# Split weights in rows of 260 elements instead of 256, in a one-core trunk kernel

## The chip, the cores and the metric

The kernel runs on one core of one Trainium2 chip. The metric is the time of one execution on the device, in microseconds (us); shorter is better. Below, PE is TensorE (matmuls; its weight loads are listed as PEld), DVE is VectorE, ACT is ScalarE, POOL is GpSimd, and SP is SyncE, whose queue issues all DMAs of this kernel. SBUF is the on-chip memory with 128 partitions, PSUM the memory that matmuls accumulate in.

## The reference: one step of a hybrid trunk layer

A batch of 288 tokens (a prompt of 256 and 8 samples of 4 new tokens) with 2048 channels passes one layer, all in float32:

```python
h = rmsnorm(x, norm1_g)
proj = h @ w_in + b_in                      # 2048 x 3072: a, gate, z
u = a * sigmoid(gate)                       # 1024 channels
c = silu(layernorm(depthwise_conv31(u), ln_g, ln_b))
d = windowed_mean(z, 2 | 4 | 8 | 16) - z    # 1024 channels in 4 groups
p = (d @ pool_w[group]) * pool_scale        # 4 x (256 x 256)
x = x + concat([c, p]) @ w_out              # 2048 x 2048
h2 = rmsnorm(x, norm2_g)
x = x + square(relu(h2 @ w_ff1)) @ w_ff2    # 2048 x 8192, 8192 x 2048
y = rmsnorm(x, norm_f)
```

The convolution and the windows also read the samples' stored history, and the new histories are outputs beside y. The three large weight arrays and pool_w come to some 175 MB, each element of which is read once.

## The kernel before

**Layout.** Activations are channel-major: channels lie on the partitions, the 288 tokens along the row. An activation tile is 128 channels by 288 tokens, 1152 bytes in each partition. Weights come in blocks of 1 MB: 1024 rows by two times 128 columns, held as `raw`, a tile of [128, 8, 256] float32 (8 values of k, 256 columns). SP's queue issues the loads in the order of use; three raw tiles rotate (`wraw`).

**The split.** TensorE's fast float32 format keeps fewer bits, so every float32 operand of a large product is cut in two parts that add up to it: hi, the rounded value, and lo, the rest. `split` (L202) does this for weights: for each half of a raw block, that is 4 values of k by 256 columns, ACT copies the half into a `whi` tile (L213), and DVE, or POOL for some of them before the MLP, subtracts: `wlo` = raw - `whi` (L214). Four `whi` and four `wlo` tiles rotate (`wspl`, L92). A tile has 4 rows of 256 elements in each partition: 4096 bytes.

**The products.** `gemm` (L223) makes 2 x 128 output channels for all tokens from n values of k. For each k and each half m of the 256 columns it issues three matmuls of 128 weight columns and 288 moving columns: hi weights times hi activations (L233), hi weights times lo activations (L234), lo weights times hi activations (L235). Each has its own weight load. Behind its matmuls `gemm` asks the generator `weight_groups` for the next group's splits, so that these run during the current group. There are 8112 such matmuls: 1152 of the input projection, 48 of the pooling groups, 768 of the output projection and 6144 of the MLP. The MLP runs in four chunks of 2048 inner channels; in each, 8 groups of w_ff1 products read the tiles `ah` and `al`, then 8 groups of w_ff2 products read 32 tiles `fh` and `fl`, which the first product's evictions made (L452 to L457). The activation tiles come from a pool of 40 rotating buffers (`actp`, L93), with two smaller sets that are reused later for parts of `ah` and `al`.

**Other work.** In the first 240 us the convolution taps on DVE (L316), the pooling windows on POOL and DVE (L347 to L362) and the LayerNorm run beside the input and output projections. `rsqrt_rows` (L177) turns sums of squares into 1 / sqrt on every partition. It is called four times. It keeps four small vectors `s[0]` to `s[3]` of 3 elements on 96 partitions (L183): DVE writes `s[0]` (L184), ACT takes the square root into `s[1]` (L185) and in two of the calls loads the next function's table with a small activation that reads a column of `s[1]` (L164), DVE takes the reciprocal into `s[2]` (L188) and makes one Newton step (L189 to L191).

**Order.** The engines' programs and all waits between them come from a tile framework: it takes the operations as written, orders them by priority and by a simulated timeline, and puts waits where two operations touch the same part of a buffer. Work inside `later()` gives way to other work that is ready. Each engine then runs its list in order.

Of the kernel before, what the change touches and what calls it, by code (L numbers as in the profile page):

```python
# [9 lines left out]
F32 = mybir.dt.float32  # L10
F32R = mybir.dt.float32r
# [3 lines left out]
PSUM = bass.MemoryType.PSUM  # L15

P = 128
D = 2048
SEQ = 256
NB, NS = 8, 4  # L20
T = SEQ + NB * NS
TB = T // 3
# [7 lines left out]
N8 = DC // P  # L30
# [9 lines left out]

# groups of two 128-column results of the input projection, in order: a convolution tile's pair
# (a_i, gate_i), or a pooling group, the widest windows first
SEQUENCE = [("conv", 0), ("conv", 1), ("conv", 2), ("conv", 3)]
# [5 lines left out]
def weight_blocks():  # L49
    """Blocks of 1024 rows and 2 x 128 columns of the weights in the order of their use:  # L50
    (array, first row, the first columns)."""
    for kind, i in SEQUENCE:
        cols = (i * P, DC + i * P) if kind == "conv" else (2 * DC + 2 * i * P, 2 * DC + (2 * i + 1) * P)
        for r in range(0, D, 1024):
            yield "w_in", r, cols
    yield "pool_w", 0, (0, P)
    for r in (DC, 0):
        for c in range(0, D, 256):
            yield "w_out", r, (c, c + P)
    for ch in range(0, DFF, FCH):  # L60
        for c in range(ch, ch + FCH, 256):
            for r in range(0, D, 1024):
                yield "w_ff1", r, (c, c + P)
        for c in range(0, D, 256):
            for r in range(ch, ch + FCH, 1024):
                yield "w_ff2", r, (c, c + P)


# of 8 lo parts, how many GpSimd computes
SHARE = {"first": 2, "second": 4, "conv": 7, "pool": 5, "pool_w": 3, "w_out": 6}  # L70

# per-channel vectors, [P, columns]: channel = column * P + partition
VEC = (("norm1_g", 16), ("b_in", 24), ("conv_b", 8), ("ln_g", 8), ("ln_b", 8), ("pool_scale", 8), ("norm2_g", 16), ("norm_f", 16))
# [9 lines left out]
def trunk_kernel(ctx: ExitStack, tc: tile.TileContext, io):  # L83
    """Activations are channel-major: [channel on the partitions, token]. Tokens: the prompt's
    256, then 8 x 4 of the samples. Every float32 operand of a large product is split exactly in
    two float32r parts (12 bits each): w x = wh xh + wh xl + wl xh, in float32 accumulation."""
    nc = tc.nc

    const = ctx.enter_context(tc.tile_pool(name="const", bufs=1))
    rowp = ctx.enter_context(tc.tile_pool(name="rowp", bufs=4))  # L90
    wraw = ctx.enter_context(tc.tile_pool(name="wraw", bufs=3))
    wspl = ctx.enter_context(tc.tile_pool(name="wspl", bufs=4))  # L92
    actp = ctx.enter_context(tc.tile_pool(name="actp", bufs=40))  # L93
    tmpp = ctx.enter_context(tc.tile_pool(name="tmpp", bufs=8))
# [7 lines left out]
    def nm(s):  # L102
        seen[s] = seen.get(s, 0) + 1
        return f"{s}{seen[s]}"

    @contextmanager
    def later(by=LATER):
        """Work that gives way to all else that is ready."""
        tc.cur_priority += by
        yield  # L110
        tc.cur_priority -= by
# [18 lines left out]

# [1 line left out]
    vec = const.tile([P, NV], F32, name="vec")  # L132
    xT = const.tile([P, KT, T], F32, name="xT")
    u_all = const.tile([P, N8, UL], F32, name="u_all")
    z_all = const.tile([P, N8, ZL], F32, name="z_all")
# [6 lines left out]
    def load(cuts=((0, 8),), x_cuts=()):  # L142
        """The next 1 MB of weights; at the start in pieces, with pieces of x between them"""
        raw = wraw.tile([P, 8, 256], F32, name=nm("wr"), tag="wr")
        src = io["w"][next(blocks)]
        for j, (k0, k1) in enumerate(cuts):
            if j < len(x_cuts):
                a, b = x_cuts[j]
                nc.sync.dma_start(xT[:, a:b, :], io["xT"][:, a:b, :])
            nc.sync.dma_start(raw[:, k0:k1, :], src[:, k0:k1, :])  # L150
        return raw
# [10 lines left out]
    def load_table(func, src):  # L162
        """The function's table is loaded once src is there."""
        nc.scalar.activation(few[: src.shape[0], :], src, func)  # L164
# [12 lines left out]
    def rsqrt_rows(parts, scale, after=None):  # L177
        """PSUM [P, T], on every partition: 1 / sqrt(scale * sum over parts and partitions + eps)."""
        pt = ms("pt", 3)
        for j in range(3):  # L180
            for n, t in enumerate(parts):
                nc.tensor.matmul(pt[:TB, j : j + 1], t[:, j * TB : (j + 1) * TB], ones[:, 0:1], start=n == 0, stop=n == len(parts) - 1)  # L182
        s = [const.tile([TB, 3], F32, name=nm("st")) for _ in range(4)]  # L183
        nc.vector.tensor_scalar(s[0], pt[:TB, 0:3], scale, EPS, op0=ALU.mult, op1=ALU.add)  # L184
        nc.scalar.activation(s[1], s[0], AF.Sqrt)  # L185
        if after is not None:
            load_table(after, s[1][:, 0:1])
        nc.vector.reciprocal(s[2], s[1])  # L188
        nc.vector.tensor_tensor(s[3], s[2], s[2], op=ALU.mult)  # L189
        nc.vector.scalar_tensor_tensor(out=s[3], in0=s[3], scalar=-0.5, in1=s[0], op0=ALU.mult, op1=ALU.mult)  # L190
        nc.vector.scalar_tensor_tensor(out=s[2], in0=s[3], scalar=1.5, in1=s[2], op0=ALU.add, op1=ALU.mult)  # L191
        dg = tmp("dg")
        for j in range(3):
            nc.vector.tensor_scalar(dg[:TB, j * TB : (j + 1) * TB], ident, s[2][:, j : j + 1], None, op0=ALU.mult)
        pr = ms("pr")
        nc.tensor.matmul(pr[:, :T], ones[:TB, :], dg[:TB, :], start=True, stop=True)
        return pr

# [1 line left out]
    turn = {"n": 0}  # L200

    def split(raw, share=0, cut=4):  # L202
        """[P, 8, 256] -> get(k, m): the parts of 128 columns; `share` of 8 on GpSimd"""
        parts = []
        for h in range(2):
            hi = wspl.tile([P, 4, 256], F32R, name=nm("whi"), tag="whi")
            lo = wspl.tile([P, 4, 256], F32R, name=nm("wlo"), tag="wlo")
            turn["n"] += share
            eng = nc.gpsimd if turn["n"] >= 8 else nc.vector
            turn["n"] %= 8  # L210
            for k in range(0, 4, cut):
                src = raw[:, 4 * h + k : 4 * h + k + cut, :]
                nc.scalar.copy(hi[:, k : k + cut, :], src)  # L213
                eng.tensor_tensor(lo[:, k : k + cut, :], src, hi[:, k : k + cut, :].bitcast(F32), op=ALU.subtract)  # L214
            parts.append((hi, lo))

        def get(k, m):
            hi, lo = parts[k // 4]
            return hi[:, k % 4, m * P : (m + 1) * P], lo[:, k % 4, m * P : (m + 1) * P]

        return get

    def gemm(banks, rhs, m_outer=False):  # L223
        """banks[m] = sum over k of w(k, m)^T rhs[k]; the next group's weights are split meanwhile"""
        n = len(rhs)
        gets = ready.pop()
        order = [(k, m) for k in range(n) for m in range(len(banks))]
        if m_outer:
            order.sort(key=lambda km: km[1])
        for k, m in order:  # L230
            (xh, xl), b = rhs[k], banks[m][:, :T]
            wh, wl = gets[k // 8](k % 8, m)
# [7 lines left out]

# [1 line left out]
    hx = []  # L242
# [8 lines left out]
    def weight_groups():  # L251
        """Per group of products, get(k, m) for each block of 8 k, in the order of the products."""
        yield [split(raw0, SHARE["first"], 2), split(raw1, SHARE["first"], 2)]
# [5 lines left out]
        for _ in range(8):  # L259
            get = split(load(), SHARE["w_out"])  # L260
# [8 lines left out]

# [1 line left out]
    scratch = z_all[:].rearrange("p k t -> p (k t)")[:, 0 : 5 * 2 * T].rearrange("p (n k t) -> p n k t", n=5, t=T)  # L271
# [15 lines left out]

# [1 line left out]
    cs = []  # L289
# [38 lines left out]

# [1 line left out]
    dd = {}  # L330
# [39 lines left out]

# [1 line left out]
    mixp = {}  # L372
# [9 lines left out]

# [1 line left out]
    pmean = ms("pmean")  # L384
# [24 lines left out]

# [1 line left out]
    for g in range(8):  # L411
# [4 lines left out]

# [1 line left out]
    x1 = []  # L418
# [20 lines left out]

# [1 line left out]
    r2 = row("r2")  # L441
# [34 lines left out]

# [1 line left out]
    rf = rsqrt_rows([ssf, qf], 1.0 / D)  # L478
# [62 lines left out]
```

## Time and profile before

| | |
|---|---|
| median of 3 runs | 1126.65 us (1126.13 to 1128.41) |
| profiled execution, first to last instruction | 1125.9 us |
| PE busy | 1094.4 us (97%), 8190 matmuls |
| DVE busy | 677.1 us (60%) |
| ACT busy | 468.7 us (42%) |
| POOL busy | 188.8 us (17%) |
| mean DMA rate | 166 GB/s |
| mean granted TensorE clock | 0.987 of full speed |

In the profile's tables a row of instructions reads: line, engine, operation, the tile written and those read (buffer numbers left out), shapes as partitions x elements, the count behind an x, then busy time in us and the mean duration of one in ns, then the idle time of that engine just before, with what ended most of it. In a table by stretches each engine has its busy time and the number of its instructions in brackets; PEclk is the clock that TensorE was granted. A timeline row begins with the start in us and the duration. The digits of a row such as "PE 7998..." are the busy tenths of 40 equal slices of the span. Matmuls are pipelined, so the durations of neighbouring ones overlap and the spacing of their starts is what counts.

### The profile page before, as it was taken

To read this page: it belongs to the slowest core of one execution; us is meant where nothing else is said; L and a number is where in the kernel's file an instruction comes from. 1 tells how busy PE (TensorE), PEld (TensorE's weight loads), DVE (VectorE), ACT (ScalarE), POOL (GpSimd) and SP (SyncE) were. 2 spreads that over 40 slices of the span, in tenths; PEclk is the share of its full clock that TensorE was granted. 3 is DMA by queue.
4 is the path that set the end of the run, shared out by engine and by line. 5 is a ranking of instruction groups with operands and counts; after the bars stand their busy time and mean duration, and the time that the engine had idled before them with its cause. 6 is when DMAs were issued, how large, how long until landed. Compare 5 with 4: busy or idle time off the path is not lost.

```text
span 1125.9 us, 19336 instructions
## 1 busy us (share of the span) xinstructions
PE 1094.4 (97%) x8190; PEld 1089.8 (97%) x8190; DVE 677.1 (60%) x983; ACT 468.7 (42%) x643; POOL 188.8 (17%) x149
## 2 busy tenths in 40 slices
PE   7998898999999999999999999999999999999995
PEld 7998898999999999999999999999999999999995
DVE  7999999788755544445555444455444445555554
ACT  6443345356544433334444333344433334444441
POOL 4789886612200000000000000000000000000000
PEclk9999998989999999999999999999999999999998
DMA  8554438534445444444445454444444454545432
GB/s 298 191 175 164 148 115 222 184 113 166 172 150 177 160 171 167 158 179 154 184 153 183 152 182 156 174 163 167 170 160 178 153 184 151 183 155 175 162 113 84
DMA packets 31910, 187.01 MB, mean 166 GB/s; under 512 B 3408, under 2 KB 7760, under 8 KB 10448
## 3 DMA queue, kind: packets, MB, share of 16 engines
q1 hardware_dynamic: 31824, 185.78, 47.0%
q8 instruction: 64, 1.05, 0.4%
q14 instruction: 22, 0.18, 0.0%
HBM read 181.49 MB, written 4.28 MB: 165 GB/s over the span
## 4 chain that ended last, share of the span: by engine, by line
PE 86%; DVE 9%; POOL 2%; issue 2%; DMA 1%; ACT 0%; SPq 0%; DVEq 0%; POOLq 0%
PE ac L233 29%; PE ac L234 28%; PE ac L235 28%; DVE pc L316 3%; DVE wlo L214 1%; POOL wlo L214 1%; DVE d L354 1%; DVE ssc L397 1%; DVE d L351 1%; DMA xT<-in_xT 1%; POOL s L347 0%; DVE d L359 0%; DVE z_all L283 0%; PE pt L182 0%; DVE xT L481 0%
## 5 line engine op out<-in xcount | busy, mean ns | idle before, releaser
L213 ACT CAST whi<-wr 128x1024 fp32r<-128x1024 f32 (+1 forms) x342 | 355.0, 1040 | 562.8 <-PE ac L234 543.6
L214 DVE TENSOR_TENSOR wlo<-wr,whi 128x1024 fp32r<-128x1024 f32 (+1 forms) x295 | 364.7, 1236 | 371.8 <-ACT whi L213 371.7
L233 PE MATMUL ac<-ah,whi 128*128 128x288 f32 x1024 | 302.7, 296 | 0.0
L233 PE MATMUL ac<-fh,whi 128*128 128x288 f32 x1024 | 302.4, 295 | 0.0
L234 PE MATMUL ac<-al,whi 128*128 128x288 f32 x1024 | 301.2, 294 | 0.0
L234 PE MATMUL ac<-fl,whi 128*128 128x288 f32 x1024 | 301.2, 294 | 0.0
L235 PE MATMUL ac<-fh,wlo 128*128 128x288 f32 x1024 | 299.3, 292 | 0.0
L235 PE MATMUL ac<-ah,wlo 128*128 128x288 f32 x1024 | 298.8, 292 | 0.0
L235 PEld LDWEIGHTS ac<-fh,wlo 128*128 128x128 f32 x1024 | 193.1, 189 | 0.0
L235 PEld LDWEIGHTS ac<-ah,wlo 128*128 128x128 f32 x1024 | 192.9, 188 | 0.0
L234 PEld LDWEIGHTS ac<-fl,whi 128*128 128x128 f32 x1024 | 192.7, 188 | 0.0
L234 PEld LDWEIGHTS ac<-al,whi 128*128 128x128 f32 x1024 | 192.4, 188 | 0.1
L233 PEld LDWEIGHTS ac<-ah,whi 128*128 128x128 f32 x1024 | 192.1, 188 | 0.1
L233 PEld LDWEIGHTS ac<-fh,whi 128*128 128x128 f32 x1024 | 192.0, 188 | 0.0
L233 PE MATMUL ac<-hh,whi 128*128 128x288 f32 x384 | 113.6, 301 | 7.7 <-DVE tg L302 6.6
L214 POOL TENSOR_TENSOR wlo<-wr,whi 128x1024 fp32r<-128x1024 f32 (+1 forms) x47 | 112.3, 2400 | 34.0 <-ACT whi L213 31.4
L234 PE MATMUL ac<-hl,whi 128*128 128x288 f32 x384 | 114.9, 301 | 3.0 <-DVE hl L246 2.9
L235 PE MATMUL ac<-hh,wlo 128*128 128x288 f32 x384 | 114.2, 301 | 1.5 <-DVE wlo L214 1.4
L316 DVE SCALAR_TENSOR_TENSOR pc<-u_all,vec,pc 128x256 f32<-128x256 f32 x232 | 100.1, 479 | 1.3
L233 PEld LDWEIGHTS ac<-hh,whi 128*128 128x128 f32 x384 | 73.3, 193 | 8.4 <-issue 7.0
L234 PEld LDWEIGHTS ac<-hl,whi 128*128 128x128 f32 x384 | 74.3, 194 | 4.1 <-DVE hl L246 4.1
L235 PEld LDWEIGHTS ac<-hh,wlo 128*128 128x128 f32 x384 | 74.1, 194 | 2.3 <-DVE wlo L214 2.2
(115 smaller groups left out, 875.5 us busy)
## 6 DMA issues: line engine op xcount, KB each, us to landing
wr<-in_w SPq DMA_DIRECT2D x167, 1024.0 KB, 4.9
xT<-in_xT SPq DMA_DIRECT2D x8, 288.0 KB, 5.7
wr<-in_w SPq DMA_DIRECT2D x8, 256.0 KB, 5.6
out_u_out<-u_all SPq DMA_DIRECT2D x1, 1208.0 KB, 8.6
out_yT<-xT SPq DMA_DIRECT2D x2, 576.0 KB, 2.9
u_all<-in_hist_c SPq DMA_DIRECT2D x8, 136.0 KB, 5.8
out_z_out<-z_all SPq DMA_DIRECT2D x1, 668.0 KB, 7.4
z_all<-in_hist_p SPq DMA_DIRECT2D x4, 152.0 KB, 4.0
```

What stands on the lines that cost most here:

```text
L213: nc.scalar.copy(hi[:, k : k + cut, :], src)
L214: eng.tensor_tensor(lo[:, k : k + cut, :], src, hi[:, k : k + cut, :].bitcast(F32), op=ALU.subtract)
L233: nc.tensor.matmul(b, wh, xh, start=k == 0, stop=False)
L234: nc.tensor.matmul(b, wh, xl, start=False, stop=False)
L235: nc.tensor.matmul(b, wl, xh, start=False, stop=k == n - 1)
L316: nc.vector.scalar_tensor_tensor(out=dst, in0=up[:, w : w + SEQ], scalar=cwv[:, w : w + 1], in1=pc, op0=ALU.mult, op1=ALU.add)
L351: nc.vector.scalar_tensor_tensor(out=d[:, w - 1 : SEQ], in0=s[:, PH + w - 1 : ZO], scalar=1.0 / w, in1=z[:, PH + w - 1 : ZO], op0=ALU.mult ...
L354: nc.vector.scalar_tensor_tensor(out=samples(d[:, SEQ:T], NS), in0=ss[:, :, PH:], scalar=1.0 / w, in1=zs[:, :, PH:], op0=ALU.mult, op1=ALU ...
L397: nc.vector.tensor_tensor(ssc, ssc, q, op=ALU.add)
```

## The change

The tiles `whi` and `wlo` get 260 elements in a row instead of 256, of which the first 256 are used. A row then takes 1040 bytes and a tile 4160, so that the starts of rows and buffers fall on all multiples of 16 bytes modulo 256. The raw tile, the transfers, the instructions and their number of elements stay as they are; the written operand of L213 and two operands of L214 are now four separate runs of 256 elements. The eight weight tiles take 512 bytes more in each partition. To make room, the four small vectors of `rsqrt_rows` become slices of one tile. Apart from these lines only comments differ.

```diff
     wspl = ctx.enter_context(tc.tile_pool(name="wspl", bufs=4))
+    WROW = 256 + 4
...
-        s = [const.tile([TB, 3], F32, name=nm("st")) for _ in range(4)]
+        st = const.tile([TB, 4, 3], F32, name=nm("st"))
+        s = [st[:, n, :] for n in range(4)]
...
-            hi = wspl.tile([P, 4, 256], F32R, name=nm("whi"), tag="whi")
-            lo = wspl.tile([P, 4, 256], F32R, name=nm("wlo"), tag="wlo")
+            hi = wspl.tile([P, 4, WROW], F32R, name=nm("whi"), tag="whi")[:, :, 0:256]
+            lo = wspl.tile([P, 4, WROW], F32R, name=nm("wlo"), tag="wlo")[:, :, 0:256]
```

## The prediction

> **What bounds the kernel now.** I read the page first, for the busy shares, the waits before the split instructions and the chain that ended last.
>
> ```profile
> span 1125.9 us, 19336 instructions
> PE   7998898999999999999999999999999999999995
> PEclk9999998989999999999999999999999999999998
> PE 86%; DVE 9%; POOL 2%; issue 2%; DMA 1%; ACT 0%; SPq 0%; DVEq 0%; POOLq 0%
> L213 ACT CAST whi<-wr 128x1024 fp32r<-128x1024 f32 (+1 forms) x342 | 355.0, 1040 | 562.8 <-PE ac L234 543.6
> L214 DVE TENSOR_TENSOR wlo<-wr,whi 128x1024 fp32r<-128x1024 f32 (+1 forms) x295 | 364.7, 1236 | 371.8 <-ACT whi L213 371.7
> ```
>
> TensorE (PE) carries 86% of the chain. From the eighth slice on it is nearly always full, at the full granted clock. ScalarE (ACT) waits 543.6 us for PE to release a `whi` buffer, and VectorE (DVE) 371.7 us for ACT. So in the long stretch the splitting engines are early, and the time is the number of matmuls times their spacing, start to start. Next I read the busy time by stretches: the cold start, the busy first part, the whole MLP, and four equal stretches of the MLP.
>
> ```profile
> core 0: us, PE busy (x) PEld busy (x) DVE busy (x) ACT busy (x) POOL busy (x), PEclk, DMA share, GB/s
> 17.20:20.40 3.20, 3.20 (x13) 3.20 (x14) 3.20 (x7) 3.20 (x8) 0.64 (x1) 0.50 1.04 417
> 40.00:200.00 160.00, 149.69 (x1094) 148.74 (x1093) 156.56 (x322) 65.48 (x94) 134.29 (x90) 0.97 0.49 164
> 301.60:1111.30 809.70, 809.70 (x6160) 809.59 (x6159) 397.04 (x470) 323.48 (x418) 1.02 (x1) 1.00 0.46 162
> 404.50:502.50 98.00, 98.00 (x745) 98.00 (x744) 45.05 (x48) 33.74 (x36) 0.00 (x0) 1.00 0.45 162
> 507.00:605.00 98.00, 98.00 (x748) 98.00 (x747) 49.42 (x60) 41.88 (x59) 0.00 (x0) 1.00 0.47 166
> 606.00:704.00 98.00, 98.00 (x748) 98.00 (x747) 45.53 (x49) 33.89 (x35) 0.00 (x0) 1.00 0.46 164
> 808.00:906.00 98.00, 98.00 (x745) 98.00 (x744) 45.53 (x49) 33.90 (x35) 0.00 (x0) 1.00 0.46 163
> ```
>
> In the MLP, 809.7 us over 6160 PE instructions is 131.4 ns each. Now the cold start, where the granted clock is 0.50; from 18.29 to 20.21 lie eight matmuls, two of them in the row "x2" left out here.
>
> ```profile
> 18.29 0.44 PE L234 MATMUL ac<-hl,whi 128*128 128x288 f32 x1
> 18.53 0.44 PE L235 MATMUL ac<-hh,wlo 128*128 128x288 f32 x1
> ...
> 20.21 0.42 PE L234 MATMUL ac<-hl,whi 128*128 128x288 f32 x1
> ```
>
> 1.92 us over eight is 240 ns. Half of that, 120 ns, is what the same 288 columns would take at the full clock if nothing else came in. They take 131.4. So about 11 ns of each of the 8112 matmuls on split weights, 89 us in all, is an excess that appears at the full clock alone. It bounds what any arrangement of addresses could win.
>
> Is that excess a matter of addresses? From the code: a `whi` or `wlo` tile has 4096 bytes in a partition, its rows 1024, a half row 512, so all weight operands start at one residue modulo 256. A moving tile has 1152 bytes, 4.5 times 256, so neighbours alternate between two residues, 128 apart. The relation "moving start minus weight start, modulo 256" has two values today, 0 and 128. In the chunks' second products `fh` and `fl` change places in this respect: their 32 tiles come out of a ring of 40 buffers, so chunks 0 and 2 have mostly `fh` on the weights' residue, chunks 1 and 3 `fl`. Of three products two move `fh`. The stretches above show just this: 745 matmuls in 98 us in chunks 0 and 2 (404.5 and 808), 748 in chunk 1 (606) at the same clock and the same load on ACT and DVE. That is 131.54 against 131.02 ns. The relation counts, by 0.5 ns between its two values.
>
> The last view is the timeline of PE behind a stall.
>
> ```profile
> 110.42 0.37 PE L233 MATMUL ac<-hh,whi 128*128 128x288 f32 x1 [2.99 <-DVE tg L302]
> ...
> 110.89 0.29 PE L233 MATMUL ac<-hh,whi 128*128 128x288 f32 x1
> 111.02 0.30 PE L234 MATMUL ac<-hl,whi 128*128 128x288 f32 x1
> 111.16 0.30 PE L235 MATMUL ac<-hh,wlo 128*128 128x288 f32 x1
> 111.29 0.30 PE L233 MATMUL ac<-hh,whi 128*128 128x288 f32 x1
> 111.43 0.31 PE L234 MATMUL ac<-hl,whi 128*128 128x288 f32 x1
> 111.57 0.30 PE L235 MATMUL ac<-hh,wlo 128*128 128x288 f32 x1
> ...
> 112.11 0.30 PE L233 MATMUL ac<-hh,whi 128*128 128x288 f32 x1
> ...
> 113.70 0.30 PE L233 MATMUL ac<-hh,whi 128*128 128x288 f32 x1
> ```
>
> The first nine matmuls from 110.89 take 1.22 us, 135.6 ns each, although nothing waits. The next twelve, from 112.11, take 1.59 us, 132.5 each. So the spacing depends on how the two streams of reads stand to each other in time too: after a disturbance it is worse, then it settles.
>
> **The change, part by part.** *Addresses of the weights.* A row becomes 1040 bytes (4 x 256 + 16), a tile 4160 (16 x 256 + 64). Row k of buffer t then starts at 64t + 16k modulo 256: sixteen residues; `wlo` starts four tiles (65 x 256) behind `whi`, on the same ones. Moving tiles keep their two residues. So the relation, constant for hundreds of matmuls today, moves by 16 bytes with every k, that is every six matmuls. No row shows the other fourteen relations. The bounds: at best the whole excess goes, -89 us; at worst PE is always as it is in the nine matmuls behind the stall, 135.6 against 131.3 (the mean of the four stretches), 4.3 ns x 8112 = +35 us. The restart rows are nearest, since there too a settled spacing is broken. If every one of the 1352 steps (8112 / 6) cost what a restart costs, 9 x 4.3 = 39 ns, that would be 52 us, above the cap of 35. But a step is 16 bytes, an eighth of the 128 that part the two known relations; I take an eighth of the cost. 52 / 8 = **+6.6 us**.
>
> The Trainium skill, "SBUF — State Buffer", section "Who interferes with whom", gives TensorE two read ports, one for the moving operand and one for the weights, and says that it never waits on anyone. By that the spacing couldn't depend on a relation of addresses, and this term would be 0 instead of +6.6; the stretches with 745 and 748 speak against it as a strict rule.
>
> *The split instructions.* Each of the 342 copies and 342 subtractions writes (the subtraction also reads) four rows instead of one run. In the MLP nothing of it shows: the idle times of 543.6 and 371.7 us before them hide it. Without that cover, between 40 and 200 us, DVE is busy 156.56 of 160 us.
>
> ```profile
> L214 DVE TENSOR_TENSOR wlo<-wr,whi 128x1024 fp32r<-128x1024 f32 x12 | 17.5, 1460 | 0.5 <-ACT whi L213 0.5
> L481 DVE TENSOR_TENSOR xT<-xT,pr 128x1152 f32<-128x1152 f32 x2 | 2.6, 1348 | 0.0
> L481 DVE TENSOR_TENSOR xT<-xT,pr 128x576 f32<-128x576 f32 x2 | 1.5, 746 | 0.0
> L481 DVE TENSOR_TENSOR xT<-xT,pr 128x288 f32<-128x288 f32 x1 | 0.5, 455 | 0.8 <-PE pr L196 0.8
> L213 ACT CAST whi<-wr 128x512 fp32r<-128x512 f32 x8 | 4.9, 608 | 1.0 <-DMA wr<-in_w 0.9
> ```
>
> L481 already reads an operand in rows (one row of 288 repeated): one row 455 ns, two 746, four 1348, about 300 for each further row, less than a row alone. I take 0. The far end: if each of three row starts cost an instruction's fixed part (ACT 608 ns for 512 elements, 1040 for 1024, so 176 ns fixed), that would be 0.53 us on each of DVE's 12 splits of this stretch, +6 us. A gain is excluded: the elements stay the same. GpSimd (POOL) does 47 of the subtractions; DVE and not POOL fills this stretch, so they get 0 too.
>
> *The four small vectors of `rsqrt_rows` in one tile.* Same instructions. A cost arises only if the reciprocal (L188) now also waits for the table load that reads a neighbouring slice.
>
> ```profile
> L188 DVE RECIPROCAL st<-st 96x3 f32<-96x3 f32 x4 | 0.7, 168 | 0.8 <-ACT st L185 0.8
> L164 ACT ACT_TABLE_LOAD x4 | 5.1, 1283 | 0.8 <-PEq L523 0.7
> L164 ACT ACTIVATE few<-st 96x1 f32<-96x1 f32 x2 | 0.4, 202 | 0.0
> ACT hh L245 <- DMA xT<-in_xT: 2.2, 2, 2.1
> ```
>
> Two of the four calls load a table: at most 2 x (1.28 + 0.20) = +3.0 us. Behind the reciprocal stand the rest of DVE's queue and the matmul L196. I take 0: `hh` reads slices of one tile that eight transfers fill and waited for transfers only twice, so waits go by slices. No DMA is added or moved on any queue.
>
> Sum: 6.6 + 0 + 0 against the profiled execution's span of 1125.9 gives 1132.5; the median of the three runs, 1126.65, stands 0.75 above it, so **1133 us**.
>
> **The rivals.** *Slower through broken settling (forecast), 0.46.* For it: the restart. Against it: it is scaled from a single kind of disturbance. 1129 to 1150 us.
>
> *Faster: today's two relations are poor ones, 0.34.* If the mean over sixteen relations lies below today's mean, PE gains on every matmul. For it: 11 ns of excess, and two relations that already differ by 0.5 ns. Against it: nothing shows a relation that is much better. Priced at three times the difference seen, 1.6 ns x 8112 = -13 us: 1114 us. It decides from a mean spacing below 131.0 ns (0.28 ns x 8112 = 2.3 us, the 0.2% that a measurement of this kernel can tell from no change).
>
> *No effect: the fourteen new relations average to the old two, 0.14.* The mean over a rotation is what two opposite points of it give, if the excess comes from two streams that pass each other a fixed number of times. 1126.6 us. This is also where the skill's rule of independent ports, quoted above, would lead.
>
> *Slower by the small terms alone, 0.06.* DVE's rows or the wait for the table: +3 to +9 us, 1130 to 1136, seen before 300 us and not in the MLP.
>
> **How the numbers follow.** Slower 0.46 + 0.06 = 0.52, same 0.14, faster 0.34. The time is the forecast's, 1133. The range has to hold both signs: down to 1110, a little past the faster rival's 1114, and up to 1150, two thirds of the way to the cap 1162 of PE always unsettled; about 0.06 is left out below and 0.1 above.
>
> **What would show it.** In the four MLP stretches of 98 us, 745 to 748 matmuls today: about 742 by the forecast, above 752 by the faster rival, 745 to 748 without effect. L213 and L214 in the MLP stay near 1.04 and 1.24 us and still wait for PE and ACT. L188 keeps its wait of 0.2 to 0.3 us a call. Cold matmuls stay at 240 ns. The prediction is wrong if spacing falls, or if the time goes in the first 300 us.

## The result and the profile after

The changed kernel takes 1133.2 us (median of 4 runs, 1130.89 to 1135.58) against 1126.42 before: 1.0059 times as long, 95% interval 1.0043 to 1.0076. It is slower, by about 6.8 us.

From the page of the changed kernel: the span, the granted clock in 40 slices, the chain by engine, and the copies and subtractions of the split (L215 and L216 are L213 and L214 of before).

```profile
span 1133.9 us, 19336 instructions
PEclk8999998989999999999999999999999999999998
PE 89%; DVE 6%; POOL 2%; issue 1%; DMA 1%; ACT 0%; SPq 0%; DVEq 0%; POOLq 0%
L215 ACT CAST whi<-wr 128x1024 fp32r<-128x1024 f32 (+1 forms) x342 | 354.7, 1038 | 568.7 <-PE ac L236 552.2
L216 DVE TENSOR_TENSOR wlo<-wr,whi 128x1024 fp32r<-128x1024 f32 (+1 forms) x295 | 364.4, 1235 | 376.8 <-ACT whi L215 376.6
L216 POOL TENSOR_TENSOR wlo<-wr,whi 128x1024 fp32r<-128x1024 f32 (+1 forms) x47 | 113.5, 2427 | 35.0 <-ACT whi L215 32.4
```

The split costs what it did: 1038 ns against 1040 on ACT, 1235 against 1236 on DVE, and on POOL, which does no subtractions in the MLP, 2427 against 2400. ACT waits longer for PE (552.2 us against 543.6), so PE has become slower, and the others wait for it. The table by stretches of the changed kernel has the whole MLP in its first row, then the four stretches of 98 us:

```profile
302.60:1119.00 816.40, 816.40 (x6158) 816.29 (x6158) 397.26 (x470) 323.23 (x418) 1.00 (x1) 1.00 0.46 160
404.50:502.50 98.00, 98.00 (x741) 98.00 (x740) 45.04 (x49) 33.78 (x35) 0.00 (x0) 1.00 0.48 168
507.00:605.00 98.00, 98.00 (x741) 98.00 (x740) 49.30 (x62) 41.85 (x59) 0.00 (x0) 1.00 0.47 166
606.00:704.00 98.00, 98.00 (x741) 98.00 (x740) 45.08 (x49) 33.85 (x35) 0.00 (x0) 1.00 0.48 166
808.00:906.00 98.00, 98.00 (x741) 98.00 (x740) 45.61 (x49) 33.20 (x36) 0.00 (x0) 1.00 0.47 162
```

The MLP takes 816.4 us instead of 809.7: +6.7 us at the same full clock, within 0.1 us of what the medians differ by. A stretch now counts 741 matmuls, where there were 745 or 748. Such a count takes in also the two or three matmuls that lie across the ends of the stretch, so 98 us divided by it comes out some 0.4 ns too small. From here on a spacing is taken from the starts in the trace: over the whole MLP 132.7 ns instead of 131.6 (132.67 and 131.55; four longer steps near the start of the MLP, which all kernels have, are left out). The difference between the chunks is gone too, since each chunk now runs through all relations. The profiled spans differ by 8.0 us. Of the rest, 1.3 us, 1.0 lies before the MLP, which starts at 302.6 instead of 301.6; the first slice had a lower granted clock in this profile (digit 8 against 9).

Each engine's instructions are the same as before, in the same order and with as many waits. As far as the medians go, the time went into the spacing of matmuls in the MLP.

### The profile page after: what moved, and what is told of

Read it like the earlier page. It is cut to its first block, busy times and chain, and to the rows that moved or that the text cites. A ratio compares the mean times of both kernels' runs of the same rounds, so it can differ in the third digit from the quotient of the medians.

```text
span 1133.9 us, 19336 instructions
## 1 busy us (share of the span) xinstructions
PE 1103.4 (97%) x8190; PEld 1098.7 (97%) x8190; DVE 673.8 (59%) x983; ACT 468.6 (41%) x643; POOL 189.9 (17%) x149
## 4 chain that ended last, share of the span: by engine, by line
PE 89%; DVE 6%; POOL 2%; issue 1%; DMA 1%; ACT 0%; SPq 0%; DVEq 0%; POOLq 0%
PE ac L237 30%; PE ac L235 29%; PE ac L236 29%; DVE pc L318 2%; POOL wlo L216 1%; DVE wlo L216 1%; DVE ssc L399 1%; DMA xT<-in_xT 1%; PE pt L183 1%; POOL s L349 1%; DVE d L353 0%; DVE d L356 0%; DVE xT L483 0%; DVE z_all L285 0%; DVE c L392 0%
## 5 line engine op out<-in xcount | busy, mean ns | idle before, releaser
L215 ACT CAST whi<-wr 128x1024 fp32r<-128x1024 f32 (+1 forms) x342 | 354.7, 1038 | 568.7 <-PE ac L236 552.2
L216 DVE TENSOR_TENSOR wlo<-wr,whi 128x1024 fp32r<-128x1024 f32 (+1 forms) x295 | 364.4, 1235 | 376.8 <-ACT whi L215 376.6
L237 PE MATMUL ac<-fh,wlo 128*128 128x288 f32 x1024 | 303.2, 296 | 0.0
L237 PE MATMUL ac<-ah,wlo 128*128 128x288 f32 x1024 | 302.8, 296 | 0.0
L216 POOL TENSOR_TENSOR wlo<-wr,whi 128x1024 fp32r<-128x1024 f32 (+1 forms) x47 | 113.5, 2427 | 35.0 <-ACT whi L215 32.4
```

What stands on the lines that cost most here:

```text
L237: nc.tensor.matmul(b, wl, xh, start=False, stop=k == n - 1)
```

## The experiments

"Relation" is, as in the prediction, the moving operand's start minus the weights' start, modulo 256. A hi activation and its lo neighbour always differ by 128, so a kernel that holds its relations has two. By the addresses in the built programs, three in four hi operands have the one in some chunks, and three in four the other in the rest.

Unless more are named, a time below is one execution. Single times of the kernel before lie between 1125.2 and 1128.7 us. The MLP itself takes 809.7, 809.7 and 809.6 us in the profiles of three kernels that hold the same relations (the kernel before and two of the runs below). So the comparisons go by the MLP.

### The relation held at other values: shifts by 32, 64 and 96 bytes

The weights stay in rows of 256; a gap ahead of the activation pool moves all activations (here by 32 bytes).

```diff
+    padp = ctx.enter_context(tc.tile_pool(name="padp", bufs=1))
+    gap = padp.tile([P, 8], F32, name="gap")     # 16 for 64 bytes, 24 for 96
+    nc.vector.memset(gap[:, 0:1], 0.0)
     actp = ctx.enter_context(tc.tile_pool(name="actp", bufs=40))
```

> A gap of 32 bytes ahead of the activation pool: weights as before, every activation 32 bytes further, so that the relation moving minus weight is constant again, 32 and 160 modulo 256 in place of 0 and 128. Theory S (settling: a constant relation is cheap, a changing one costs): as before, 745 to 748 matmuls in the MLP stretches of 98 us, 1126 to 1128 us. Theory V (each relation has a price of its own; a run's time is the mean over the relations that it uses): in the changed kernel three matmuls whose hi operand has relation 32 took 399.0 ns, at 160 they took 400.6, against 393.5 to 396.6 before; 133.3 ns a matmul, about 735 in 98 us, about 1140 us.

> The same with 64 bytes: constant relations 64 and 192. Theory S: 745 to 748 matmuls in 98 us, 1126 to 1128 us. Theory V: in the changed kernel three matmuls took 398.4 ns at 64 and 395.6 at 192; weighted, 132.2 ns a matmul, about 741 in 98 us, about 1132 us.

> The same with 96 bytes: constant relations 96 and 224. Theory S: 745 to 748 matmuls in 98 us, 1126 to 1128 us. Theory V: in the changed kernel three matmuls took 399.0 ns at 96 and 400.2 at 224; 133.2 ns a matmul, about 735 in 98 us, about 1140 us.

The figures of the changed kernel that the expectations use, such as 390.3 ns, are worked out from the starts in its trace: three matmuls of one k and one half, averaged over the MLP by the relation of the hi operand. The expected counts are 98 us divided by a spacing, so the tables count two or three more for the same spacing.

Measured: 1129.3, 1135.3 and 1133.3 us, beside 1125.7 for the kernel before. From the tables by stretches, the second products of chunks 0 and 1 (404.5 and 606), first for the shift by 32, then 64, then 96:

```profile
404.50:502.50 98.00, 98.00 (x741) 98.00 (x740) 44.66 (x47) 33.14 (x35) 0.00 (x0) 1.00 0.46 163
606.00:704.00 98.00, 98.00 (x747) 98.00 (x746) 45.51 (x49) 33.93 (x35) 0.00 (x0) 1.00 0.46 164
```

```profile
404.50:502.50 98.00, 98.00 (x739) 98.00 (x739) 45.20 (x49) 33.94 (x35) 0.00 (x0) 1.00 0.46 162
606.00:704.00 98.00, 98.00 (x741) 98.00 (x740) 45.54 (x49) 33.32 (x35) 0.00 (x0) 1.00 0.48 170
```

```profile
404.50:502.50 98.00, 98.00 (x739) 98.00 (x738) 44.49 (x47) 32.81 (x35) 0.00 (x0) 1.00 0.47 163
606.00:704.00 98.00, 98.00 (x742) 98.00 (x741) 44.95 (x50) 33.82 (x35) 0.00 (x0) 1.00 0.47 166
```

A relation that never changes costs as much at 64 and 192 (739 and 741) as the change does (741). So a relation need not change to be dear: theory S falls. Theory V is right in kind, but not for each value: where the hi operand has 160 (the shift by 32, mostly in chunk 1) it foresaw 400.6 ns for three matmuls, 133.5 each, and the starts of this run give 131.2.

### The parities exchanged: a shift by 128 bytes

The same gap with 32 elements.

> The same with 128 bytes: relations 0 and 128 as before, with the two activation parities exchanged. Both theories: what chunks 0 and 2 had in their second products, chunks 1 and 3 now have and the first products too, so 748 matmuls in 98 us from 404.5 and from 808, 745 from 507 and from 606; about 2 us slower than before, 1128 us, if the price hangs on the relation alone. If it hung on absolute addresses of the activations, the pattern would stay as it was.

Measured: 1131.8 us. The four stretches of this kernel:

```profile
404.50:502.50 98.00, 98.00 (x748) 98.00 (x747) 44.74 (x48) 34.12 (x36) 0.00 (x0) 1.00 0.46 163
507.00:605.00 98.00, 98.00 (x745) 98.00 (x744) 48.91 (x60) 41.87 (x59) 0.00 (x0) 1.00 0.48 167
606.00:704.00 98.00, 98.00 (x742) 98.00 (x741) 45.52 (x49) 33.97 (x35) 0.00 (x0) 1.00 0.46 163
808.00:906.00 98.00, 98.00 (x742) 98.00 (x741) 45.20 (x49) 33.78 (x35) 0.00 (x0) 1.00 0.48 169
```

The exchange shows in chunk 0 (748 instead of 745) and in chunk 1's first products (745 instead of 748). But chunk 1's second products have 742 instead of the 745 expected, and chunk 2's 742 instead of 748. So the same relation can run at more than one spacing. The starts show when it went over: where the hi operand has 128, a matmul takes 131.1 to 131.4 ns up to 606 us and 132.1 to 132.2 from there to the end; where it has 0, 132.2 to 132.3 and then 132.6 or more. The MLP takes 813.8 us instead of 809.7: 4.1 more with the same two relations, of which the exchange was to explain some 2. What picks the one or the other spacing is open.

### Weights and activations moved together

```diff
+    padp = ctx.enter_context(tc.tile_pool(name="padp", bufs=1))
+    gap = padp.tile([P, 16], F32, name="gap")
+    nc.vector.memset(gap[:, 0:1], 0.0)
     wspl = ctx.enter_context(tc.tile_pool(name="wspl", bufs=4))
```

> The gap of 64 bytes stands ahead of the weight tiles instead of behind them, so that weights and activations move up together: weights at residue 192 instead of 128, relations 0 and 128 as before. If the relation alone sets the price: 745 matmuls in the stretches from 404.5 and 808, 748 from 507 and 606, about 1126 us, as before. If the weights' own residue mattered (in the changed kernel matmuls on weights at residue 192 took 132.4 ns): some 740 in 98 us and about 1133 us, as with the gap of 64 bytes behind the weights.

Measured: 1127.6 us, beside 1127.9 for the kernel before on that chip.

```profile
404.50:502.50 98.00, 98.00 (x745) 98.00 (x744) 44.63 (x47) 33.71 (x36) 0.00 (x0) 1.00 0.46 163
507.00:605.00 98.00, 98.00 (x748) 98.00 (x747) 49.41 (x60) 41.84 (x59) 0.00 (x0) 1.00 0.48 167
606.00:704.00 98.00, 98.00 (x748) 98.00 (x747) 45.32 (x49) 34.03 (x36) 0.00 (x0) 1.00 0.47 163
808.00:906.00 98.00, 98.00 (x745) 98.00 (x744) 45.12 (x49) 33.73 (x35) 0.00 (x0) 1.00 0.46 162
```

The old pattern to the matmul. A gap of 64 bytes behind the weights costs five to seven matmuls in each of the four stretches, the same gap ahead of them none. The price hangs on the relation of the two operands, not on where either lies.

### The odd multiples of 16: the other eight relations, held

Tiles start at multiples of 32 bytes, so the weights become slices of one tile with 16 bytes left free at its start. The order of the first 300 us moves a little by this; the MLP is compared.

```diff
-    wspl = ctx.enter_context(tc.tile_pool(name="wspl", bufs=4))
+    wspl = ctx.enter_context(tc.tile_pool(name="wspl", bufs=1))
+    wall = wspl.tile([P, 8 * 1024 + 8], F32R, name="wall")
+    wn = {"n": 0}
...
-            hi = wspl.tile([P, 4, 256], F32R, name=nm("whi"), tag="whi")
-            lo = wspl.tile([P, 4, 256], F32R, name=nm("wlo"), tag="wlo")
+            b = [4 + 1024 * (4 * j + wn["n"] % 4) for j in range(2)]
+            hi, lo = [wall[:, a : a + 1024].rearrange("p (k c) -> p k c", c=256) for a in b]
+            wn["n"] += 1
```

> The eight weight tiles become slices of one tile whose first 16 bytes stay unused; rows stay 256 elements apart. Constant relations 16 and 144. Theory S (settling) is out after the shifts by 64 and 96; what is open is whether the price of a relation when it is held is the price that it had when the changed kernel passed through it (V), or whether only the mean over many relations carries over (M). V: 390.3 ns for three matmuls at 144 and 396.3 at 16, 130.9 ns a matmul, about 749 in 98 us, about 1121 us, faster than before. M: anything from 131.2 to 133.3 ns a matmul, 1126 to 1141 us.

> The same with a gap of 32 bytes ahead of the activations: constant relations 48 and 176. V: 399.3 ns at 176 and 395.5 at 48, 132.6 ns a matmul, about 739 in 98 us, about 1135 us. M: 131.2 to 133.3 ns, 1126 to 1141 us.

> The same with a gap of 64 bytes: constant relations 80 and 208. V: 399.8 ns at 208 and 398.2 at 80, 133.1 ns a matmul, about 736 in 98 us, about 1138 us. M: 131.2 to 133.3 ns, 1126 to 1141 us.

> The same with a gap of 96 bytes: constant relations 112 and 240. V: 400.7 ns at 240 and 400.9 at 112, 133.6 ns a matmul, about 734 in 98 us, about 1142 us. M: 131.2 to 133.3 ns, 1126 to 1141 us. Together with the kernel before and the four shifts these make all sixteen relations; their mean is the price of passing through all of them without a cost of the passing itself, to be held against the changed kernel's 132.7 ns.

Measured: 1126.4, 1139.1, 1137.3 and 1148.9 us, beside 1127.7 for the kernel before. The same two stretches, for relations 16 and 144, 48 and 176, 80 and 208, 112 and 240:

```profile
404.50:502.50 98.00, 98.00 (x744) 98.00 (x744) 44.66 (x47) 33.66 (x35) 0.00 (x0) 1.00 0.46 164
606.00:704.00 98.00, 98.00 (x749) 98.00 (x749) 44.89 (x48) 34.03 (x36) 0.00 (x0) 1.00 0.47 164
```

```profile
404.50:502.50 98.00, 98.00 (x743) 98.00 (x742) 45.56 (x49) 33.86 (x35) 0.00 (x0) 1.00 0.48 169
606.00:704.00 98.00, 98.00 (x739) 98.00 (x738) 45.55 (x49) 33.30 (x35) 0.00 (x0) 1.00 0.45 161
```

```profile
404.50:502.50 98.00, 98.00 (x738) 98.00 (x738) 44.62 (x49) 33.78 (x35) 0.00 (x0) 1.00 0.47 167
606.00:704.00 98.00, 98.00 (x740) 98.00 (x739) 44.82 (x49) 33.86 (x35) 0.00 (x0) 1.00 0.47 166
```

```profile
404.50:502.50 98.00, 98.00 (x729) 98.00 (x728) 45.09 (x49) 33.00 (x35) 0.00 (x0) 1.00 0.47 165
606.00:704.00 98.00, 98.00 (x729) 98.00 (x728) 44.16 (x47) 32.82 (x34) 0.00 (x0) 1.00 0.47 166
```

Now all sixteen relations have been held. By kernel, the mean count of the two stretches, the MLP from its first start to its last, and the mean spacing of the starts in it:

| relations held | mean count in 98 us | MLP, us | ns a matmul |
|---|---|---|---|
| 16 and 144 | 746.5 | 807.5 | 131.2 |
| 0 and 128 (before) | 746.5 | 809.7 | 131.6 |
| 32 and 160 | 744 | 812.2 | 132.0 |
| 96 and 224 | 740.5 | 816.5 | 132.7 |
| 64 and 192 | 740 | 817.2 | 132.8 |
| 48 and 176 | 741 | 817.6 | 132.8 |
| 80 and 208 | 739 | 818.1 | 132.9 |
| 112 and 240 | 729 | 830.0 | 134.9 |
| mean of the eight | 740.8 | 816.1 | 132.6 |
| all in turn (the change) | 741 | 816.5 | 132.7 |
| 0 and 128, exchanged (shift by 128) | 745 | 813.8 | 132.2 |

The change takes what the eight kernels take on the mean, 816.5 us against 816.1, and against 816.6 with the shift by 128 in the place of the kernel before. So on the mean, passing from one relation to the next adds nothing that can be seen, and the kernel before happened to hold one of the two cheapest pairs. For a single relation this isn't so. By the relation of the hi operand, a held one costs from 130.4 ns (144) to 135.1 (240); passed in the changed kernel, the cheapest and the dearest cost 130.1 (144) and 133.6 (112), 240 costs 133.6 too, and 160 costs 133.5 where it costs 131.2 held. Theory V missed here (131.2 ns for the first kernel where it foresaw 130.9, 134.9 for the last where it foresaw 133.6); theory M, that only the mean carries over, held except that its band was too narrow: 134.9 ns lies above its 133.3. Why the single prices shift and their mean does not, no run shows.

The clock matters too. At the start of the run with 112 and 240 the granted clock was 0.50; fourteen matmuls lie between these two rows of its timeline:

```profile
18.96 0.44 PE L234 MATMUL ac<-hl,wall 128*128 128x288 f32 x1
...
22.32 0.44 PE L234 MATMUL ac<-hl,wall 128*128 128x288 f32 x1
```

3.36 us over fourteen is 240 ns, as in the kernel before. At half clock the worst relation costs nothing.

### Every hi operand at the cheapest relation

In the run with 16 and 144 the chunks differ: 749 against 744. Where hi mostly has 144, it is cheap. So hi and lo become one tile, and hi has the same residue everywhere.

```diff
-    def act(name, **kw):
-        return actp.tile([P, T], F32R, name=nm(name), **(kw or {"tag": "act"}))
+    def act2(name, **kw):      # half as many buffers in each set
+        t = actp.tile([P, 2, T], F32R, name=nm(name), **(kw or {"tag": "act"}))
+        return t[:, 0, :], t[:, 1, :]
```

To this come the one tile for the weights and a gap of 128 bytes ahead of the activations. The convolution's results, which share buffers with later activations, are paired in the same way.

> Each hi and lo activation pair becomes one tile of 2304 bytes (9 x 256), hi first, so that every hi operand keeps one residue; with the weights 16 bytes up and a gap of 128 bytes ahead of the activations, every hi operand has relation 144 and every lo operand 16, in all 8112 matmuls. V (a held relation has its price): 130.4 ns a matmul instead of 131.6, about 751 in 98 us, 1.14 ns x 8112 = 9 us less than before, about 1117 us. If something other than the relation made the price in the run with 16 and 144, the spacing stays at 131.2 to 131.6 and the time near 1126 us. The tiles' release in pairs moves the order of the first 240 us a little, by plus or minus 2 us.

Measured: 1121.1 us (median of 4) against 1126.3 (median of 13), 0.9953 times as long (95% interval 0.9937 to 0.9970), faster than both kernels. Two stretches of this kernel, then three rows of PE's waits, first of this kernel and then of the kernel before:

```profile
404.50:502.50 98.00, 98.00 (x757) 98.00 (x756) 45.43 (x49) 34.70 (x36) 0.00 (x0) 1.00 0.46 166
606.00:704.00 98.00, 98.00 (x757) 98.00 (x756) 45.37 (x50) 33.08 (x34) 0.00 (x0) 1.00 0.48 172
```

```profile
PE ac L233 <- DVE tg L302: 12.6, 3, 6.0
PE ac L235 <- DVE wall L214: 4.1, 3, 2.5
PE ac L234 <- DVE hh L246: 0.3, 2, 0.2
```

```profile
PE ac L233 <- DVE tg L302: 9.8, 3, 3.6
PE ac L234 <- DVE hl L246: 2.9, 3, 1.3
PE ac L235 <- DVE wlo L214: 2.0, 3, 0.8
```

The starts are 130.0 ns apart in every stretch, a little better than the 130.4 expected, and the MLP takes 800.1 us instead of 809.7. The time is 4 us above what was expected, nevertheless. A part of this lies before the MLP: the three waits come to 17.0 us against 14.7 before (`hh` in the third row is the pair's tile, so it is the old wait for `hl`). The MLP starts at 302.8 us, against 301.6 in the kernel before and 299.5 in the run below, which was taken on the same chip. So the new order of the first part gives back between 1 and 3 us. The profiled execution is the fastest of the four (1119.3 us); what the others add is not placed.

### The vectors of rsqrt_rows alone

> The change's other part alone: the four small vectors of rsqrt_rows become slices of one tile, the weights keep rows of 256. All buffers behind move down by 256 bytes, so no residue changes. If waits go by slices: as before, 1126.4 us within 0.2%. If the reciprocal now waits for the table load: up to 3.0 us more, 1129.4 us, and the idle time before L188 grows from 0.8 to some 3.8 us.

The diff is the one shown under the change, for `s` only. Measured: 1126.1 us (median of 10) against 1126.3, ratio 0.9994 (0.9985 to 1.0003). The reciprocal in this run:

```profile
L188 DVE RECIPROCAL st<-st 96x3 f32<-96x3 f32 x4 | 0.7, 172 | 0.8 <-ACT st L185 0.8
```

Its wait is the old 0.8 us. This part costs nothing that can be seen; the reciprocal doesn't wait for the table load.

## Why the prediction was right or wrong

**The time** came out as forecast, 1133 us, and by the stage that was named: in the MLP, in the spacing of matmuls, without a wait behind it.

**Addresses of the weights: the size was right and the reason wrong.** The step held that a relation which moves every six matmuls keeps PE unsettled, and priced it at an eighth of a restart, +6.6 us. The shifts by 64 and 96 bytes hold their relations and are as slow as the change; the mean of the eight kernels that hold, 132.6 ns, is the change's spacing within 0.1. No cost of moving shows. What the step left out is that the relations differ in price when they are held, from 131.2 to 134.9 ns for a pair, and that today's pair is among the cheapest. The eighth was a guess of scale that happened to meet the number: that was luck. The sum was also made over 8112 matmuls; in the medians the MLP's 6144 carried it (6.7 us), while before the MLP DVE, busy 156.56 us of 160, probably leaves PE less to lose. And its 131.3 ns was a stretch divided by its count; the starts in the four stretches give 131.7, with which the same sum comes to about +6.

**The excess of 11 ns over 120** held as a reading. A part of it depends on addresses, at the full clock alone: the arrangements that were run spread from 130.0 to 134.9 ns. The 10 ns that the best one keeps over 120 are not explained.

**The restart rows** were taken as evidence of settling in time. They still show that the same two relations can run at more than one spacing, and the shift by 128 shows it again, this time lasting: its MLP went over at 606 us and stayed. But they were no measure of a step in address.

**The two relations of before** were read rightly (745 and 748 go with which operand has which relation: moved together, the pattern stays; exchanged, chunk 0 and the first products of chunk 1 exchange). The faster rival had the right mechanism, a price for each relation, with the wrong sign: it asked whether today's two were poor, and they were good. The rival without effect fell with its premise: the price isn't the same at all sixteen. Two opposite points don't give the mean: at 0 and 128 they give 131.6, at 112 and 240 134.9.

**The Trainium skill's rule** in "SBUF — State Buffer", section "Who interferes with whom", that TensorE has two independent read ports and never waits on anyone, doesn't hold as a rule on time here: of two kernels that differ in a gap of 96 bytes alone, the one runs at 131.2 ns and the other at 134.9. Whether a port is what they differ by, no run shows. The Trainium skill's "TensorE: Matmul & The Clock Gate", section "Back-to-back issue gap", gives N / 1.2 ns cold and N / 2.4 + 2.5 warm as the gap of matmuls in isolation; for 288 columns that is, as an estimate, 240 and 122.5. The cold figure agrees (240); no run here reached the warm one, the best held 130.0.

**The split instructions and the small vectors** were taken at 0 and nothing of them shows: 1038 and 1235 ns a split, and a ratio of 0.9994 for the vectors.

## What to carry to other kernels

When matmuls run back to back, measure their spacing by stretches and compare stretches that differ only in which buffers they read; a difference at the same clock and the same load points to addresses. Move one pool by a small gap to test it, then both together. If addresses count, don't spread them: here a spread bought the mean. Hold each relation in turn, compare several stretches or a whole stage, since one relation can run at more than one spacing, and keep the best for the operand that is moved most.

## What the runs showed of the hardware

Three things were new to me. The spacing of 128 x 128 by 288 matmuls depends on the moving operand's start minus the weights' start modulo 256, in the steps of 16 bytes that were tried: between 130.0 and 134.9 ns on the mean of the MLP at the full clock, and not at half clock (240 ns in the two kernels looked at, which hold 0 and 128, and 112 and 240). Moving both together by 64 bytes changes nothing. And one relation can run at more than one spacing: with hi mostly on the weights' residue, the shift by 128 ran at 745 in 98 us in one stretch and at 742 in the next. That the two streams of reads meet in the memory would fit the first two, but no run here shows where they meet; this stays open.
